# A sum of reciprocals: the last four rows' Exp one row at a time, and the first load in two transfers

## The chip, the cores and the metric

The kernel runs on one core of a Trainium2 chip. The metric is the device time of one execution in microseconds (us). The kernel before takes 171.85 us, the median of three runs that lie between 171.72 and 171.97 us. The profile comes from one further execution, whose span on the core is 169.9 us.

## The reference

The input `x` has the shape 32 x 512 x 1024, float32, all positive: 16,384 rows of 1024 numbers, 67.1 MB. For each row the reciprocals are summed.

```python
x = np.abs(np.random.randn(32, 512, 1024)).astype(np.float32) + 1e-6

def reference(x):
    return np.sum(1.0 / x, axis=-1).astype(np.float32)
```

The 16,384 rows lie as 128 rows on each of the 128 partitions. In the rest of this text, "row c" means the c-th row of every partition, c from 0 to 127: one such row is 128 x 1024 numbers.

## The kernel before

[...] the kernel halves their number. It pairs element i of the first half of a row (call it a) with element i of the second half (b), and uses

1/a + 1/b = (a + b) / (a b).

For each row it forms the 512 products a b, and their reciprocals on ScalarE as exp(-ln(a b)). A power of two, S, is multiplied in twice so that it cancels. What remains is the sum over the pairs of (a + b) times the reciprocal. There are two ways to get it, and the kernel uses both to share the work between engines:

- a row of the "ring" kind: VectorE multiplies the whole row of 1024 by the 512 reciprocals, used twice, and sums up. The reciprocals are the tile `rc` in PSUM.
- a row of the "s" kind: TensorE forms a + b first, as two matmuls with the identity that are accumulated in PSUM (tile `s`), and VectorE multiplies and sums only 512 pairs. The reciprocals are written over the products in the tile `ps`.

The products a b come from GpSimd. For 11 rows TensorE copies the second half to PSUM (tile `b`) and VectorE forms the product.

The work is cut into chunks of two rows. In `(m, e, v)`, m is the number of rows, e how many are of the "s" kind, and v how many products VectorE forms. Chunk A has two ring rows, B two s rows, C two s rows of which VectorE forms one product.

```python
R = 40                                  # rows of the ring buffer in SBUF
A, B, C = (2, 0, 0), (2, 2, 0), (2, 2, 1)
LOADS = [[A, B, A, B], [A, B, A, C]] * 5 + [[A, B], [A, C]] * 4 + [[A], [B], [A], [C]] * 2
```

The loads therefore take eight rows at a time at first, then four, then two. The last four loads are rows 120 and 121 (A), 122 and 123 (B), 124 and 125 (A), 126 and 127 (C).

```python
def sum_rows(c, xc, pr, sm, rc):
    m, e = xc.shape[1], len(sm)
    for j in range(e, m):                           # ring rows
        row = xc[:, j, :].rearrange("p (h e) -> p h e", h=2)
        sum_row(
            c + j,
            row,
            rc[:, j - e, :].unsqueeze(1).to_broadcast([P, 2, H]),
            pr[:, e : e + 2, :] if j == e and m - e > 1 else None,
        )
    for j in reversed(range(e)):                    # s rows, the last one first
        sum_row(c + j, pr[:, j, :], sm[j])

waiting = None
c0 = 0
for chunks in LOADS:
    n = sum(m for m, _, _ in chunks)
    xt = ring[:, c0 % R : c0 % R + n, :]
    keep(nc.sync.dma_start(out=xt, in_=x_v[:, c0 : c0 + n, :]))
    ...                       # for v rows: matmul into b, VectorE product into pr
    for (m, e, v), pr in zip(chunks, made):
        xc = xt[:, q : q + m, :]
        ...                   # GpSimd: the products of rows v to m, into pr
        ...                   # TensorE: s = first half + second half, for e rows
        if waiting:
            sum_rows(*waiting)                      # the chunk before this one
        keep(nc.scalar.activation(out=pr, in_=pr, func=Ln, scale=S))
        rc = None
        if e < m:
            rc = rpool.tile([P, m - e, H], f32, tag="rc")
            i = nc.scalar.activation(out=rc, in_=pr[:, e:, :], func=Exp, scale=-1.0)
            keep(i)
        if e:
            r = pr[:, :e, :]
            keep(nc.scalar.activation(out=r, in_=r, func=Exp, scale=-1.0))
        waiting = c0 + q, xc, pr, sm, rc
        q += m
    c0 += n
sum_rows(*waiting)
nc.sync.dma_start(out=out_v, in_=sums)
```

`keep` holds the instructions of an engine in the order of the program. `sum_row` is one VectorE instruction that multiplies, sums, and writes the elementwise result somewhere; the fourth argument of `sum_row` is that place. For the first ring row of a chunk the place is the tile of products, which Exp has read by then.

Of the kernel before, what the change touches and what calls it, by code (L numbers as in the profile page):

```python
# [1 line left out]

# [6 lines left out]


@with_exitstack
def kernel(
    ctx: ExitStack,
    tc: tile.TileContext,
    x: bass.AP,
    out: bass.AP,
):

    nc = tc.nc
    f32 = mybir.dt.float32
    P = 128  # L30
    D = 1024
    H = D // 2
    F = 128

    R = 40

    S = float(2**17)

    A, B, C = (2, 0, 0), (2, 2, 0), (2, 2, 1)
    LOADS = [[A, B, A, B], [A, B, A, C]] * 5 + [[A, B], [A, C]] * 4 + [[A], [B], [A], [C]] * 2

    Ln = mybir.ActivationFunctionType.Ln
    Exp = mybir.ActivationFunctionType.Exp
    mult = mybir.AluOpType.mult
    plus = mybir.AluOpType.add

    x_v = x.flatten_outer_dims().rearrange("(p f) d -> p f d", p=P)
    out_v = out.flatten().rearrange("(p f) -> p f", p=P)  # L50

    act_sets = list(get_activation_tables(nc.m.arch).keys())
    nc.scalar.add_instruction(  # L53
        mybir.InstLoadActFuncSet(
            name=nc.get_next_instruction_name(),
            act_func_set_id=act_sets.index("natural_log_exp_and_others"),
            ins=[],
            outs=[],
        )
    )  # L60

    ppool = ctx.enter_context(tc.tile_pool(name="ppool", bufs=4))
    opool = ctx.enter_context(tc.tile_pool(name="opool", bufs=1))
    spool = ctx.enter_context(
        tc.tile_pool(name="spool", bufs=3, space=bass.MemoryType.PSUM)
    )
    bpool = ctx.enter_context(
        tc.tile_pool(name="bpool", bufs=1, space=bass.MemoryType.PSUM)
    )
    rpool = ctx.enter_context(  # L70
        tc.tile_pool(name="rpool", bufs=2, space=bass.MemoryType.PSUM)
    )

    ring = opool.tile([P, R, D], f32)
    sums = opool.tile([P, F], f32)
    ident = opool.tile([P, P], f32)
    make_identity(nc, ident)
    keep = tc.keep_in_program_order

    def add(bank, *halves):  # L80
        for k, half in enumerate(halves):
            i = nc.tensor.matmul(  # L82
                bank,
                lhsT=ident,
                rhs=half,
                start=k == 0,
                stop=k == len(halves) - 1,
            )
            keep(i)

    def sum_row(c, row, fac, out=None):
        i = nc.vector.tensor_tensor_reduce(  # L92
            out=row if out is None else out,
            in0=row,
            in1=fac,
            scale=S,
            scalar=0.0,
            op0=mult,
            op1=plus,
            accum_out=sums[:, c : c + 1],  # L100
# [5 lines that stand above are left out]
        for j in range(e, m):  # L106
            row = xc[:, j, :].rearrange("p (h e) -> p h e", h=2)
            sum_row(
                c + j,
                row,  # L110
                rc[:, j - e, :].unsqueeze(1).to_broadcast([P, 2, H]),
                pr[:, e : e + 2, :] if j == e and m - e > 1 else None,
            )
        for j in reversed(range(e)):
            sum_row(c + j, pr[:, j, :], sm[j])

    waiting = None
    c0 = 0
    for chunks in LOADS:
        n = sum(m for m, _, _ in chunks)  # L120
        xt = ring[:, c0 % R : c0 % R + n, :]
        keep(nc.sync.dma_start(out=xt, in_=x_v[:, c0 : c0 + n, :]))  # L122

        made, q = [], 0
        for m, e, v in chunks:
            pr = ppool.tile([P, m, H], f32, tag="ps" if e else "pr")
            for j in range(v):
                b = bpool.tile([P, H], f32, tag="b")
                add(b, xt[:, q + j, H:])
                i = nc.vector.tensor_tensor(  # L130
                    out=pr[:, j, :], in0=xt[:, q + j, :H], in1=b, op=mult
                )
                keep(i)
            made.append(pr)
            q += m

        q = 0
        for (m, e, v), pr in zip(chunks, made):
            xc = xt[:, q : q + m, :]
            if v < m:  # L140
                i = nc.gpsimd.tensor_tensor(  # L141
                    out=pr[:, v:, :], in0=xc[:, v:, :H], in1=xc[:, v:, H:], op=mult
                )
                keep(i)
            sm = []
            for j in range(e):
                s = spool.tile([P, H], f32, tag="s")
                add(s, xc[:, j, :H], xc[:, j, H:])
                sm.append(s)
            if waiting:  # L150
                sum_rows(*waiting)
            keep(nc.scalar.activation(out=pr, in_=pr, func=Ln, scale=S))  # L152
            rc = None
            if e < m:
                rc = rpool.tile([P, m - e, H], f32, tag="rc")
                i = nc.scalar.activation(  # L156
                    out=rc, in_=pr[:, e:, :], func=Exp, scale=-1.0
                )
                keep(i)
            if e:  # L160
                r = pr[:, :e, :]
                keep(nc.scalar.activation(out=r, in_=r, func=Exp, scale=-1.0))  # L162
            waiting = c0 + q, xc, pr, sm, rc
            q += m
        c0 += n
    assert c0 == F, c0
    sum_rows(*waiting)

    nc.sync.dma_start(out=out_v, in_=sums)


# [1 line left out]
_INS = ['x']  # L173
_OUTS = [((32, 512), 'float32')]


# [23 lines left out]
```

## Time and profile before

| | |
|---|---|
| time, median of 3 | 171.85 us |
| span of the profiled execution | 169.9 us |
| TensorE busy | 131.7 us (77%) |
| VectorE busy | 122.3 us (72%) |
| ScalarE busy | 133.9 us (79%) |
| GpSimd busy | 138.3 us (81%) |
| read from HBM | 67.11 MB, in 26 loads of 4, 2 and 1 MB |
| share of the chain that ended last | transfers of x 78%, GpSimd's products 11%, VectorE 3%, ScalarE 2% |

An engine's busy share is an average over the whole execution. The chain that ended last is followed back from the last instruction, at each step to what released it. The views used below are the page's DMA row (the busy share of the 16 DMA engines in 40 equal slices of the span, in tenths), windows (busy time of each engine in chosen stretches, with the granted clock of TensorE, the DMA share and GB/s at the end of the line), and timelines (instructions of one engine in order of time). In the profile PE is TensorE, DVE is VectorE, ACT is ScalarE, POOL is GpSimd. In a timeline, neighbouring instructions of the same kind are put together, and "x2" counts them; a float32 matmul shows as two records.

### The profile page before, as it was taken

How to read it: one execution, taken by the hardware profiler on the slowest of the kernel's cores; microseconds unless marked ns; L12 is line 12 of the kernel's file. 1: busy time of each engine (PE TensorE's matmuls, PEld its weight loads, DVE VectorE, ACT ScalarE, POOL GpSimd, SP SyncE). 2: the span in 40 equal slices, each digit the busy share in tenths (PEclk: the TensorE clock that was granted, in tenths of full speed). 3: DMA queues.
4: the chain of work that ended last, by engine and by line, in shares of the span. 5: the costliest groups of instructions: out<-in, count | busy, mean ns of one | idle time of the engine just before them, and what ended most of it. 6: DMA issues, size and time to landing. Idle time of an engine off the chain costs nothing.

```text
span 169.9 us, 1267 instructions
## 1 busy us (share of the span) xinstructions
PE 131.7 (77%) x278; PEld 50.5 (30%) x278; DVE 122.3 (72%) x267; ACT 133.9 (79%) x129; POOL 138.3 (81%) x70
## 2 busy tenths in 40 slices
PE   0008999786988789784997869789999999888790
PEld 0003433331332233231432323224334342333230
DVE  0000777767987577767777679778989898889883
ACT  3002989978887987958889787999999988999890
POOL 1008999699996999689996998999999889998920
PEclk9999999999999999999999999999999999999999
DMA  6999999999999999999999999999999999999400
GB/s 208 409 455 409 463 409 455 409 463 401 463 411 447 424 440 420 432 434 424 440 424 440 424 397 434 424 428 426 432 428 432 424 413 417 422 420 424 187 0 15
DMA packets 3894, 67.24 MB, mean 396 GB/s; under 512 B 432, under 2 KB 560, under 8 KB 560
## 3 DMA queue, kind: packets, MB, share of 16 engines
q1 hardware_dynamic: 3888, 67.18, 92.9%
q8 instruction: 2, 0.03, 0.1%
q14 instruction: 4, 0.03, 0.0%
HBM read 67.11 MB, written 0.07 MB: 395 GB/s over the span
## 4 chain that ended last, share of the span: by engine, by line
DMA 78%; POOL 11%; DVE 3%; ACT 2%; issue 2%; SPq 1%; POOLq 0%; DVEq 0%
DMA ring<-in_x_dram 78%; POOL pr L141 11%; DVE pr L92 2%; DVE ring L92 1%; ACT pr L152 1%; ACT rc L156 1%; SPq L122 1%; POOLq L141 0%; DVE sums L92 0%; DVEq L92 0%; DVEq L195 0%
## 5 line engine op out<-in xcount | busy, mean ns | idle before, releaser
L141 POOL TENSOR_TENSOR pr<-ring 128x1024 f32<-128x1024 f32 x64 | 137.6, 2189 | 23.6 <-DMA ring<-in_x_dram 23.3
L82 PE MATMUL s<-ring,ident 128*128 128x512 f32 x256 | 122.4, 616 | 32.5 <-DVE sums L92 16.6
L152 ACT ACTIVATE pr<-pr 128x1024 f32<-128x1024 f32 x64 | 67.4, 1053 | 28.7 <-POOL pr L141 28.5
L82 PEld LDWEIGHTS s<-ring,ident 128*128 128x128 f32 x256 | 47.0, 194 | 105.3 <-issue 63.1
L92 DVE CUSTOM_DVE_ANT_1 pr<-ring,rc 128x1024 f32<-128x1024 f32 x32 | 39.1, 1221 | 44.6 <-ACT rc L156 44.6
L92 DVE CUSTOM_DVE_ANT_0 pr<-pr,s 128x512 f32<-128x512 f32 x64 | 41.3, 683 | 0.2
L92 DVE CUSTOM_DVE_ANT_1 ring<-ring,rc 128x1024 f32<-128x1024 f32 x32 | 38.9, 1216 | 0.0
L162 ACT ACTIVATE pr<-pr 128x1024 f32<-128x1024 f32 x32 | 33.8, 1058 | 1.0
L156 ACT ACTIVATE rc<-pr 128x1024 f32<-128x1024 f32 x32 | 32.9, 1028 | 1.0
L82 PE MATMUL b<-ring,ident 128*128 128x512 f32 x22 | 12.0, 626 | 1.4 <-DMA ring<-in_x_dram 1.4
L92 DVE DVE_READ_ACCUMULATOR2_ANT sums<- 128x1 f32 x128 | 10.6, 83 | 0.0
L130 DVE TENSOR_TENSOR pr<-ring,b 128x512 f32<-128x512 f32 x11 | 7.5, 683 | 0.1
L82 PEld LDWEIGHTS b<-ring,ident 128*128 128x128 f32 x22 | 3.5, 188 | 9.0 <-DMA ring<-in_x_dram 7.6
L53 ACT ACT_TABLE_LOAD x1 | 1.3, 1283 | 0.7 <-PEq L184 0.7
masks.py:197 POOL MEMSET ident<- 128x128 f32 x1 | 0.2, 204 | 0.3 <-POOLq L184 0.3
masks.py:199 POOL TENSOR_SCALAR_AFFINE_SELECT ident<-ident 128x128 f32<-128x128 f32 x1 | 0.3, 292 | 0.1
L184 POOL MEMSET const-float32-0.0<- 128x1 f32 x1 | 0.1, 98 | 0.2 <-issue 0.2
L184 POOL MEMSET const-uint8-127<- 128x1 uint8 x1 | 0.1, 103 | 0.0
L184 POOL MEMSET const-bfloat16-1.0<- 128x1 bf16 x1 | 0.1, 101 | 0.0
L184 POOL MEMSET const-float32-1.0<- 128x1 f32 x1 | 0.1, 98 | 0.0
## 6 DMA issues: line engine op xcount, KB each, us to landing
ring<-in_x_dram SPq DMA_DIRECT2D x10, 4096.0 KB, 37.8
ring<-in_x_dram SPq DMA_DIRECT2D x8, 2048.0 KB, 37.0
ring<-in_x_dram SPq DMA_DIRECT2D x8, 1024.0 KB, 28.3
out_dram<-sums SPq DMA_DIRECT2D x1, 64.0 KB, 1.5
```

The costliest lines, as they stand in the source:

```text
L53: nc.scalar.add_instruction(mybir.InstLoadActFuncSet(name=nc.get_next_instruction_name(), act_func_set_id=act_sets.index("natural_log_exp_ ...
L82: i = nc.tensor.matmul(bank, lhsT=ident, rhs=half, start=k == 0, stop=k == len(halves) - 1,)
L92: i = nc.vector.tensor_tensor_reduce(out=row if out is None else out, in0=row, in1=fac, scale=S, scalar=0.0, op0=mult, op1=plus, accum_out ...
L122: keep(nc.sync.dma_start(out=xt, in_=x_v[:, c0 : c0 + n, :]))
L130: i = nc.vector.tensor_tensor(out=pr[:, j, :], in0=xt[:, q + j, :H], in1=b, op=mult)
L141: i = nc.gpsimd.tensor_tensor(out=pr[:, v:, :], in0=xc[:, v:, :H], in1=xc[:, v:, H:], op=mult)
L152: keep(nc.scalar.activation(out=pr, in_=pr, func=Ln, scale=S))
L156: i = nc.scalar.activation(out=rc, in_=pr[:, e:, :], func=Exp, scale=-1.0)
L162: keep(nc.scalar.activation(out=r, in_=r, func=Exp, scale=-1.0))
L184: nc = _bacc.Bacc("TRN2", target_bir_lowering=False, num_devices=1)
```

## The change

It has two parts that have nothing to do with each other.

The first is for the end of the kernel. In the last two chunks, rows 124 to 127, ScalarE forms Exp of one row at a time where it took both rows of a chunk in one instruction, so that VectorE can begin with a row when its own reciprocals are there. For rows 126 and 127 the last row comes first, as VectorE takes them in this order. As Exp of row 125 still has to read its products when VectorE works on row 124, VectorE then writes the elementwise result of row 124 over the row itself and not over the products.

The second is for the start. The first load, of eight rows, is issued as two transfers: partitions 0 to 15 and then partitions 16 to 127. The first transfer is to begin moving data sooner[...]. All later loads stay whole.

```diff
+    SINGLE = 124
...
-                rc[:, j - e, :].unsqueeze(1).to_broadcast([P, 2, H]),
-                pr[:, e : e + 2, :] if j == e and m - e > 1 else None,
+                rc[j - e].unsqueeze(1).to_broadcast([P, 2, H]),
+                pr[:, e : e + 2, :] if j == e and e + 1 < m and c < SINGLE else None,
...
-        keep(nc.sync.dma_start(out=xt, in_=x_v[:, c0 : c0 + n, :]))
+
+        for p0, p1 in ((0, 16), (16, P)) if c0 == 0 else ((0, P),):
+            i = nc.sync.dma_start(out=xt[p0:p1], in_=x_v[p0:p1, c0 : c0 + n, :])
+            keep(i)
...
-            rc = None
-            if e < m:
-                rc = rpool.tile([P, m - e, H], f32, tag="rc")
-                i = nc.scalar.activation(
-                    out=rc, in_=pr[:, e:, :], func=Exp, scale=-1.0
+
+            step = 1 if c0 + q >= SINGLE else m
+            rc = []
+            for j in range(e, m, step):
+                to = min(j + step, m)
+                r = rpool.tile([P, to - j, H], f32, tag="rc")
+                keep(
+                    nc.scalar.activation(
+                        out=r, in_=pr[:, j:to, :], func=Exp, scale=-1.0
+                    )
                 )
-                keep(i)
-            if e:
-                r = pr[:, :e, :]
+                rc += [r[:, l, :] for l in range(to - j)]
+            for to in range(e, 0, -step):
+                r = pr[:, max(to - step, 0) : to, :]
                 keep(nc.scalar.activation(out=r, in_=r, func=Exp, scale=-1.0))
```

## The prediction, made before the changed kernel was run

> **What bounds the kernel now.** I read the page's DMA row first, then the chain that ended last, then the windows of both ends, then each engine's timeline in the last 7 us, since the change touches only the first load and the last four rows.
>
> ```profile
> DMA  6999999999999999999999999999999999999400
> HBM read 67.11 MB, written 0.07 MB: 395 GB/s over the span
> 1.20:1.70 0.50, 0.00 (x0) 0.00 (x0) 0.00 (x0) 0.50 (x1) 0.10 (x1) 1.00 0.00 0
> 1.70:2.00 0.30, 0.00 (x0) 0.00 (x0) 0.00 (x0) 0.30 (x1) 0.00 (x0) 1.00 3.33 874
> 2.00:2.40 0.40, 0.00 (x0) 0.00 (x0) 0.00 (x0) 0.01 (x1) 0.00 (x0) 1.00 0.60 164
> 2.40:2.70 0.30, 0.00 (x0) 0.00 (x0) 0.00 (x0) 0.00 (x0) 0.00 (x0) 1.00 2.25 655
> 23.10:158.60 135.50, 116.20 (x251) 44.42 (x251) 110.25 (x243) 119.82 (x116) 124.57 (x58) 1.00 1.00 428
> 158.60:160.60 2.00, 1.35 (x4) 0.28 (x2) 2.00 (x3) 1.87 (x2) 1.90 (x2) 1.00 0.28 115
> ```
>
> The DMA digits are 9 from the second slice until the data is in: the kernel is bound by its load stream, 428 GB/s in the middle (last column; the column before it is the DMA share, in which a packet counts in the stretch where it starts). The first load is a packet of 32 KB per partition, 128 packets on 16 engines. Bytes by starting stretch: 874 GB/s x 0.30 us = 262 KB, which is 8 packets; 164 x 0.40 = 66 KB, 2 packets; 655 x 0.30 = 197 KB, 6 packets. So the 16 engines start between 1.70 and 2.70 us: ten early, six 0.3 to 0.9 us after the earliest. At the other end the DMA share is 0.28 in 158.60 to 160.60: some engines are done while a few still run, and those few set the last landing.
>
> The timelines of GpSimd, of VectorE and of TensorE (start us, duration us, and in brackets what ended the wait):
>
> ```profile
> 13.45 9.31 POOL L141 TENSOR_TENSOR pr<-ring 128x1024 f32<-128x1024 f32 x4 [12.15 <-DMA ring<-in_x_dram]
> 23.14 4.70 POOL L141 TENSOR_TENSOR pr<-ring 128x1024 f32<-128x1024 f32 x2 [0.38 <-DMA ring<-in_x_dram]
> ...
> 162.26 0.69 DVE L130 TENSOR_TENSOR pr<-ring,b 128x512 f32<-128x512 f32 x1
> 163.32 1.22 DVE L92 CUSTOM_DVE_ANT_1 pr<-ring,rc 128x1024 f32<-128x1024 f32 x1 [0.37 <-ACT rc L156]
> ...
> 165.61 0.08 DVE L92 DVE_READ_ACCUMULATOR2_ANT sums<- 128x1 f32 x1
> 165.84 0.69 DVE L92 CUSTOM_DVE_ANT_0 pr<-pr,s 128x512 f32<-128x512 f32 x1
> ...
> 161.10 1.13 PE L82 MATMUL b<-ring,ident 128*128 128x512 f32 x2 [1.16 <-DMA ring<-in_x_dram]
> 162.06 3.60 PE L82 MATMUL s<-ring,ident 128*128 128x512 f32 x8
> ```
>
> The first load is in at 13.45, the second at 23.14, 9.69 us later, which for 4.19 MB is 433 GB/s. The first took 13.45 - 9.69 = 3.76 us more, of which 0.74 passes before its issue: the start of the stream is what the split is aimed at. At the end the chain runs through GpSimd 158.77, Ln 161.17, Exp 162.26, then VectorE's two rows. But TensorE ends its sums for the last two rows at 162.06 + 3.60 = 165.66, and VectorE's next instruction, which needs the last of them (the sums are consumed last row first), starts at 165.84. VectorE had ended its previous row at 165.69. So two paths arrive 0.03 us apart, and both are released by landings, at 158.7 and 161.1.
>
> [...] The trace of before has no transfer of under 128 partitions[...].
>
> **The change, part by part.**
>
> Exp of rows 124 and 125. [...] VectorE is busy with its product for row 126 until 162.95, so row 124 starts near 162.95 instead of 163.32: 0.37 us earlier, and rows 124 and 125 end near 165.3. [...] But the next VectorE instruction still needs TensorE's sum at 165.66, which no part of this change moves. So about 0.33 of the 0.37 us turns into a wait for TensorE. I leave 0.05 us of gain[...].
>
> Exp of rows 126 and 127. [...] VectorE wants them at 165.8 and 166.4: nothing gained, nothing lost. Row 124's product now goes to its own place in the ring, not to the other buffer; the two forms take 1221 and 1216 ns: no difference.
>
> The split. One more issue of some 0.4 us (the first takes 0.38) is hidden, since an engine's first packet keeps it busy about 1.2 us and more. The first transfer needs one packet for each engine in place of eight. If the stagger of up to 0.9 us is the time in which the packets of an engine after the other are made, it shrinks to about 0.1 us, and the six late engines gain 0.3 to 0.8 us, the others nothing. The stream is without gaps, so an engine keeps what it gained to its last packet. What counts is whether the few engines that land last at 161.1 are among the late starters; the view does not name engines. Half of that, 0.45 us, is my choice.
>
> Sum: 171.85 - 0.45 - 0.05 = 171.35 us.
>
> **The rivals.**
>
> Rival 1, **SBUF ports**: [...] Result 174.7 to 179. [...] The profile of before cannot decide. I give it one chance in four.
>
> Rival 2, **the split is hidden**: the engines that end last are early starters that lost time in mid-stream. Then the landings stay where they are, and only the 0.05 us at the end is left: 171.8. For it: the early group is ten of 16. I give it one in four.
>
> Rival 3, **the Exp split is worth its full 0.37 us**, if TensorE's modelled end is late by so much. Against it: VectorE idled only 0.15 us before 165.84, hence this wait is short now, but its release would not come earlier. With it the sum is 171.0.
>
> **Range and chances.** Without port trouble the time lies between 170.8 (full stagger and part of the Exp) and 171.9. The port rival makes a long upper tail. I choose 170.8 to 177.0, wide upward for that reason alone. 2% is 3.4 us: faster by that has no source in the profile (0.02); slower needs the full port rival (0.24); the rest is the same (0.74).
>
> **What would show it.** Windows of the first microseconds: bytes of all 16 first packets starting in 1.7 to 2.0 means the stagger step is right. First product of GpSimd at 12.9 to 13.5 means no port trouble; at 16 or later, port trouble; and the last TensorE product at 161.1 moves by what the stream won or lost. In the last 5 us: [...] row 124 on VectorE 0.35 us earlier relative to the last landing; and its first product with s still 4.7 us after TensorE's last start for b, with a larger gap before it. If that gap doesn't grow and the product moves earlier, the step that binds it to TensorE is wrong. The prediction is wrong as a whole if the first load's landing moves by more than 1 us.

## The result, and the profile after

The changed kernel takes 180.79 us (median of 4 runs, 180.41 to 181.59) against 171.83 for the kernel before: 1.0527 times as long, with a 95% interval of 1.0489 to 1.0565. It is slower by 9.0 us, more than the predicted range allowed.

The page's DMA rows of the kernel after (busy share of the 16 engines in tenths and GB/s, in 40 slices of 4.5 us), and its list of DMA issues (size, and median us from issue to landing):

```profile
DMA  8989999999999999999999999999999999999500
GB/s 117 235 235 242 308 403 440 455 403 433 462 403 420 462 411 433 451 411 427 440 440 425 425 442 396 414 440 433 412 433 433 422 422 412 422 423 423 225 0 15
...
ring<-in_x_dram SPq DMA_DIRECT2D x1, 3584.0 KB, 21.2
ring<-in_x_dram SPq DMA_DIRECT2D x1, 512.0 KB, 7.1
```

The GB/s row of the kernel before, in slices of 4.2 us:

```profile
GB/s 208 409 455 409 463 409 455 409 463 401 463 411 447 424 440 420 432 434 424 440 424 440 424 397 434 424 428 426 432 428 432 424 413 417 422 420 424 187 0 15
```

Here the reader sees a trap: the engines are as busy as before (8 and 9 in the first five slices), yet move 117 to 308 GB/s where they moved 208 to 463. Busy here is "a packet is under way", not "data flows at full speed". From the sixth slice on the stream runs as before (403 to 462 GB/s in slices 6 to 20, where it was 401 to 463). The timeline of GpSimd after shows when the first and the second load are in (start, duration, and in brackets the wait before it and what ended it):

```profile
22.52 9.31 POOL L145 TENSOR_TENSOR pr<-ring 128x1024 f32<-128x1024 f32 x4 [21.21 <-DMA ring<-in_x_dram]
32.15 4.71 POOL L145 TENSOR_TENSOR pr<-ring 128x1024 f32<-128x1024 f32 x2 [0.32 <-DMA ring<-in_x_dram]
```

The first load is in at 22.52 where it was 13.45: 9.07 us later. The second follows after 9.63 us (9.69 before). So the whole loss lies within the first load, and nothing later makes it good. Windows after, in the stretches that the prediction used (DMA share and GB/s at the end):

```profile
1.70:2.00 0.30, 0.00 (x0) 0.00 (x0) 0.00 (x0) 0.30 (x1) 0.00 (x0) 1.00 9.37 1311
2.00:2.40 0.40, 0.00 (x0) 0.00 (x0) 0.00 (x0) 0.02 (x1) 0.00 (x0) 1.00 0.53 82
2.40:2.70 0.30, 0.00 (x0) 0.00 (x0) 0.00 (x0) 0.00 (x0) 0.00 (x0) 1.00 2.34 328
```

1311 x 0.30 us = 393 KB, 12 first packets; then 1 and 3. It was 8, 2 and 6: more engines do start early. At the other end, VectorE and TensorE after:

```profile
170.96 0.69 DVE L134 TENSOR_TENSOR pr<-ring,b 128x512 f32<-128x512 f32 x1
171.66 1.22 DVE L93 CUSTOM_DVE_ANT_1 ring<-ring,r 128x1024 f32<-128x1024 f32 x1
...
174.50 0.69 DVE L93 CUSTOM_DVE_ANT_0 pr<-pr,s 128x512 f32<-128x512 f32 x1 [0.47 <-PE s L83]
...
169.79 1.12 PE L83 MATMUL b<-ring,ident 128*128 128x512 f32 x2 [1.18 <-DMA ring<-in_x_dram]
170.75 3.60 PE L83 MATMUL s<-ring,ident 128*128 128x512 f32 x8
```

Row 124 (at 171.66) follows the product of row 126 without a gap. Before, VectorE waited 0.37 us there. But now it waits 0.47 us for TensorE before row 127. From TensorE's start for the last landing to that product it is 174.50 - 169.79 = 4.71 us; before it was 165.84 - 161.10 = 4.74.

### The profile page after: what moved, and what is told of

Read it like the earlier page. It is cut to its first block, busy times and chain, and to the rows that moved or that the text cites. A ratio compares the mean times of both kernels' runs of the same rounds, so it can differ in the third digit from the quotient of the medians.

```text
span 178.8 us, 1271 instructions
## 1 busy us (share of the span) xinstructions
PE 131.6 (74%) x278; PEld 50.1 (28%) x278; DVE 122.3 (68%) x267; ACT 134.1 (75%) x131; POOL 138.5 (77%) x70
## 4 chain that ended last, share of the span: by engine, by line
DMA 80%; POOL 9%; PE 3%; issue 2%; ACT 1%; DVE 1%; SPq 1%; DVEq 0%; POOLq 0%
DMA ring<-in_x_dram 80%; POOL pr L145 9%; PE s L83 2%; ACT pr L156 1%; SPq L125 1%; DVE ring L93 1%; PE b L83 1%; DVE pr L93 0%; DVEq L204 0%; ACT pr L171 0%; POOLq L145 0%; DVE sums L93 0%; ACT r L164 0%; DVEq L93 0%
## 5 line engine op out<-in xcount | busy, mean ns | idle before, releaser
L156 ACT ACTIVATE pr<-pr 128x1024 f32<-128x1024 f32 x64 | 67.4, 1052 | 37.4 <-POOL pr L145 37.2
L93 DVE CUSTOM_DVE_ANT_1 pr<-ring,r 128x1024 f32<-128x1024 f32 x31 | 37.9, 1222 | 52.8 <-ACT r L164 52.8
L93 DVE CUSTOM_DVE_ANT_1 ring<-ring,r 128x1024 f32<-128x1024 f32 x33 | 40.1, 1217 | 0.0
L171 ACT ACTIVATE pr<-pr 128x1024 f32<-128x1024 f32 (+1 forms) x33 | 33.9, 1031 | 1.0
L164 ACT ACTIVATE r<-pr 128x1024 f32<-128x1024 f32 (+1 forms) x33 | 33.0, 1001 | 1.0
```

Of the source, the lines that this page charges most:

```text
L93: i = nc.vector.tensor_tensor_reduce(out=row if out is None else out, in0=row, in1=fac, scale=S, scalar=0.0, op0=mult, op1=plus, accum_out ...
L164: nc.scalar.activation(out=r, in_=pr[:, j:to, :], func=Exp, scale=-1.0)
```

## The experiments

The first question was which part costs, and by what mechanism. The first theory was that the rate of a transfer depends on which partitions it reaches; the prediction and the expectations speak of ports. The ports are the author's assumption about the cause: no trace of this case shows one, and what the runs can show is partitions and rates. The rivals were two transfers as such, the uneven cut, and the reading side in HBM. Each edit is to the kernel before, where nothing else is said. Times of single packets of 32 KB are read from the runs' traces.

**The split alone.**

```diff
-        keep(nc.sync.dma_start(out=xt, in_=x_v[:, c0 : c0 + n, :]))
+        for p0, p1 in ((0, 16), (16, P)) if c0 == 0 else ((0, P),):
+            i = nc.sync.dma_start(out=xt[p0:p1], in_=x_v[p0:p1, c0 : c0 + n, :])
+            keep(i)
```

> Only the first load is split (16 and 112 partitions), Exp as before. If the split alone makes the loss: 180.8 us, first product of GpSimd at 22.5 us. If the two parts of the change work on each other: clearly less than 180 us.

Measured: 181.36 us, ratio 1.0523 (1.0478 to 1.0568). The split makes the whole loss. Its window of the start is the clearest for the stagger:

```profile
1.70:2.00 0.30, 0.00 (x0) 0.00 (x0) 0.00 (x0) 0.30 (x1) 0.00 (x0) 1.00 11.71 1638
```

1638 x 0.30 us = 491 KB: 15 of 16 first packets start within 0.3 us. The purpose of the split is reached, and GpSimd's first product still comes at 23.03, 9.6 us late in this trace.

**Two transfers by rows.**

```diff
+        for f0, f1 in ((0, 4), (4, 8)) if c0 == 0 else ((0, n),):
+            ... out=xt[:, f0:f1, :], in_=x_v[:, c0 + f0 : c0 + f1, :]
```

> The first load in two transfers as well, but by rows: four rows and four rows, each on all 128 partitions. If the loss comes from the partitions that a transfer reaches (theory of the ports): no loss, 171.5 to 172.2 us, second half landed at 13.4. If two transfers in place of one are what costs: several us slower, 175 or more.

Measured: 172.10 us, ratio 1.0005 (0.9982 to 1.0029). Two transfers in place of one cost nothing if each has all 128 partitions. The rival "two transfers as such" falls. GpSimd's product of the second half:

```profile
13.07 4.68 POOL L145 TENSOR_TENSOR pr<-ring 128x1024 f32<-128x1024 f32 x2 [0.22 <-DMA ring<-in_x_dram]
```

So the whole load is in 0.38 us earlier than before (13.45), and the time is no shorter: TensorE's last product for `b` starts at 161.09, where it was 161.10.

**Two halves of the partitions.** The pieces are `((0, 64), (64, P))`.

> The first load in two transfers of 64 partitions (0 to 63, 64 to 127)[...]. Theory of the ports: [...] the load takes twice 9.7 us, the first product of GpSimd comes at about 23.2 us and the time is about 181.5 us. If it is the uneven cut (1 and 7 packets to an engine) or the small first transfer that costs: about 172 us.

Measured: 182.37 us, ratio 1.0606 (1.0583 to 1.0629), first product of GpSimd at 23.96. An even cut loses more than the uneven one: 182.37 us against 181.36. The window over the load:

```profile
3.60:23.90 20.30, 0.00 (x0) 0.00 (x0) 0.00 (x0) 0.00 (x0) 0.00 (x0) 1.00 0.97 213
```

The whole load before:

```profile
3.60:13.40 9.80, 0.00 (x0) 0.00 (x0) 0.00 (x0) 0.00 (x0) 0.00 (x0) 1.00 1.00 431
```

213 GB/s is half of 431. In the trace 89 of the load's 128 packets of 32 KB take 2.5 to 2.6 us, where in the whole load most take 1.21.

**The same cut with another source.** The transfers of 16 and 112 partitions read the first 1024 rows of x, one after the other; the first eight rows of every partition then hold sums of other rows than the reference's.

```diff
+            near = x.flatten_outer_dims()[0:1024].rearrange("(p f) d -> p f d", p=P)
+            for p0, p1 in ((0, 16), (16, P)):
+                keep(nc.sync.dma_start(out=xt[p0:p1], in_=near[p0:p1]))
```

> Split of 16 and 112 partitions as in the change, but the first load reads other rows of x: the first 1024 rows one after the other, 32 KB from partition to partition in HBM where it was 512 KB (the first eight rows of every partition are then sums of other rows than the reference's). If the loss is on the side of SBUF (ports): 180.8 us as with the split alone. If it is on the side of HBM, from 16 engines that read at a distance of 512 KB in step: about 172 us.

Measured: 180.90 us, ratio 1.0518 (1.0491 to 1.0545), first product at 22.49. Where the data lies in HBM made no difference. The distance of 512 KB between the partitions' data is not the cause.

**The split in mid-stream.** The same cut at rows 24 to 31.

```diff
+        for p0, p1 in ((0, 16), (16, P)) if c0 == 24 else ((0, P),):
```

> The split of 16 and 112 partitions at the fourth load (rows 24 to 31) in place of the first. Theory of the ports: the stream stands just as long, some 9 us, for the load is slow wherever it lies: 180 to 181 us, because nothing later in the stream makes the time good. If the loss belongs to the start (first bytes, empty queues): about 172 us.

Measured: 184.35 us, ratio 1.0731 (1.0712 to 1.0750). It isn't the start that matters. The loss is larger than expected, 12.5 us. GpSimd's timeline shows where:

```profile
35.46 9.33 POOL L143 TENSOR_TENSOR pr<-ring 128x1024 f32<-128x1024 f32 x4 [4.06 <-DVE sums L92]
54.72 7.00 POOL L143 TENSOR_TENSOR pr<-ring 128x1024 f32<-128x1024 f32 x3 [9.94 <-DMA ring<-in_x_dram]
```

The same two before:

```profile
32.92 9.34 POOL L141 TENSOR_TENSOR pr<-ring 128x1024 f32<-128x1024 f32 x4 [1.52 <-DMA ring<-in_x_dram]
42.63 8.26 POOL L141 TENSOR_TENSOR pr<-ring 128x1024 f32<-128x1024 f32 x4 [0.37 <-DMA ring<-in_x_dram]
```

The first bracket after names VectorE, but the load ahead of the cut was itself in no earlier: its last piece lands at 35.32 us in the trace. So the load with the cut takes 19.26 us from the one before it (9.71 without the cut), which is 9.55 us lost, and the load ahead of it is 2.54 us later already; the remaining 0.4 us were not traced. In the trace the last five packets of that load take 1.5 to 2.5 us instead of 1.21. The small transfer may hold them up, but that was not shown. Of the 16-partition transfer's packets, eight take 4.6 to 4.9 us here, four times 1.21, and eight take 3.3 to 4.1.

**Three pieces, the first of them from the middle.** The pieces are `((32, 96), (0, 32), (96, P))`.

> The first load in three transfers: partitions 32 to 95, then 0 to 31, then 96 to 127. [...] Theory of the ports: the 64 in the middle go at the full rate, 2.1 MB in some 4.9 us, the other two at half, 1.05 MB in 4.9 us each; first product of GpSimd at about 18.3 us and the time about 176.8 us. If any transfer of fewer than 128 partitions is slow (the halves went at half rate): the load takes about 19.5 us as with the halves, first product near 23 us, time near 182 us.

Measured: 179.09 us, ratio 1.0412 (1.0372 to 1.0453). The load's stretches:

```profile
3.60:7.00 3.40, 0.00 (x0) 0.00 (x0) 0.00 (x0) 0.00 (x0) 0.00 (x0) 1.00 0.95 405
7.00:12.80 5.80, 0.00 (x0) 0.00 (x0) 0.00 (x0) 0.00 (x0) 0.00 (x0) 1.00 1.12 266
12.80:18.50 5.70, 0.00 (x0) 0.00 (x0) 0.00 (x0) 0.00 (x0) 0.00 (x0) 1.00 0.92 218
```

This is the run that decides. 64 partitions from 32 to 95 go at close to the full rate, 405 GB/s in 3.60 to 7.00 against 431 for the whole load before: after the first, their packets take 1.2 to 1.4 us in the trace. In the same kernel the 32 at either end go at half rate, 218 GB/s in 12.80 to 18.50: 53 of their 64 packets take 2.3 to 2.6 us (the middle stretch above mixes the tail of the fast piece with the slow one). So "fewer than 128 partitions" is not slow in itself; which partitions they are decides, in this kernel. First product at 19.61, expected 18.3; the time is 2.3 us over the expected 176.8. A little of that is the start: the first packets begin at 2.16 us instead of 1.75. The traced execution was the shortest of the four, 177.86 us.

**The other order.** The pieces are `((16, P), (0, 16))`.

> The same two transfers in the other order, 112 partitions (16 to 127) first and then 16 (0 to 15). Theory of the ports: the 112 are as slow as before[...], and the 16 take four times a packet's 1.21 us, so the loss is of the same kind, 7 to 10 us, 179 to 182 us. If a small transfer at the very start is what holds the queues up: 172 to 173 us.

Measured: 181.84 us, ratio 1.0567 (1.0521 to 1.0612), first product at 22.90. The list of DMA issues:

```profile
ring<-in_x_dram SPq DMA_DIRECT2D x1, 3584.0 KB, 18.6
```

The 112 partitions are in at 0.74 + 18.6 = 19.3 us, with no small transfer ahead of them; seven eighths of a whole load would be in at 13.45 - 9.69 / 8 = 12.2 (an estimate from the landings before). The packets of the 16 take 3.3 to 4.5 us. Both pieces are slow in either order.

**Exp alone.** The second question was the end. This is the change with its first load whole.

```diff
-        for p0, p1 in ((0, 16), (16, P)) if c0 == 0 else ((0, P),):
+        for p0, p1 in ((0, P),):
```

(Here the lines taken away are those of the changed kernel.)

> Only Exp of the last four rows one at a time; the first load whole. If TensorE's last sum holds VectorE back (the step in the prediction): 171.75 to 171.85 us, VectorE's wait before its first product with s of row 127 grows to about 0.5 us. If Exp was the bound: 171.4 to 171.5 us.

Measured: 171.88 us against 171.81, ratio 1.0006 (0.9999 to 1.0012). Nothing is gained. VectorE's timeline:

```profile
163.25 1.22 DVE L93 CUSTOM_DVE_ANT_1 ring<-ring,r 128x1024 f32<-128x1024 f32 x1
164.40 1.22 DVE L93 CUSTOM_DVE_ANT_1 ring<-ring,r 128x1024 f32<-128x1024 f32 x1
...
166.07 0.69 DVE L93 CUSTOM_DVE_ANT_0 pr<-pr,s 128x512 f32<-128x512 f32 x1 [0.45 <-PE s L83]
166.68 0.68 DVE L93 CUSTOM_DVE_ANT_0 pr<-pr,s 128x512 f32<-128x512 f32 x1
```

**Exp, and row 126 before row 127.** To show that TensorE's last sum holds the end, take away what makes VectorE need it first. This is an edit to the Exp-only kernel.

```diff
-        for j in reversed(range(e)):
+        for j in range(e) if c >= SINGLE else reversed(range(e)):
             sum_row(c + j, pr[:, j, :], sm[j])
...
-            for to in range(e, 0, -step):
-                r = pr[:, max(to - step, 0) : to, :]
+            for j in range(0, e, step):
+                r = pr[:, j : min(j + step, e), :]
```

> As the Exp-only kernel, and in the last chunk row 126 comes before row 127, on ScalarE and on VectorE, in the order in which TensorE makes their sums. If TensorE's last sum is the bound, row 126 no longer waits for it: VectorE runs through, and the end comes about 0.45 us earlier, 171.4 us. If Exp split alone has gained already, or the end is set elsewhere: no difference to the Exp-only kernel.

Measured: 171.23 us, ratio 0.9969 (0.9958 to 0.9981). It beats both kernels, by 0.6 us and by 9.6. VectorE's timeline:

```profile
163.19 1.22 DVE L93 CUSTOM_DVE_ANT_1 ring<-ring,r 128x1024 f32<-128x1024 f32 x1
...
164.33 1.22 DVE L93 CUSTOM_DVE_ANT_1 ring<-ring,r 128x1024 f32<-128x1024 f32 x1
...
165.48 0.68 DVE L93 CUSTOM_DVE_ANT_0 pr<-pr,s 128x512 f32<-128x512 f32 x1
...
166.08 0.68 DVE L93 CUSTOM_DVE_ANT_0 pr<-pr,s 128x512 f32<-128x512 f32 x1
```

The wait is gone: row 126 starts as soon as row 125 is done, and the last product starts at 166.08 where it was 166.68 in the Exp-only kernel.

**The order alone.** `for j in range(e) if c >= 124 else reversed(range(e))` in the kernel before, Exp whole.

> The kernel before with row 126 before row 127 at the end, Exp not split. Here VectorE is free at 165.69 and TensorE done at 165.66: only the start after the wait can gain, 0.1 to 0.2 us, 171.65 to 171.75 us. If TensorE were the whole bound of the end without any help of Exp: 0.4 us or more.

Measured: 171.57 us, ratio 0.9990 (0.9981 to 0.9999). In its trace row 126 is taken first, at 165.59, where row 127 started at 165.84. Alone, the order is worth some 0.2 us and Exp nothing; together 0.6 us. Each removes one of the two paths that arrived at the same time.

## Why the prediction was wrong, point by point

**What bounds the kernel: right.** The load stream is the bound, and what it loses at its start (9.07 us) comes out at the end (9.0 us).

**The stagger: right in part.** Eight of the 16 first packets started after 2.00 us before, four in the changed kernel and one in the run with the split alone; the prediction's own sign was all 16 by 2.00. The step that followed, "an engine keeps what it gained to its last packet", took each engine's speed as given. It is not: the first packets, which took 1.6 to 2.2 us before, take 2.8 to 4.5 us in the changed kernel. Nor is a gain at the start sure to reach the end: the 0.38 us of the cut by rows did not.

**The choice against the port rival: this is the step that failed.** The prediction named the rival, gave it one chance in four, and put its central time on the other side: the first load 0.45 us earlier, where it came 9.07 us later. Its range ended at 177.0, inside the rival's own 174.7 to 179. What spoke for the other side was the author's assumption that partitions are tied to engines, so that a small transfer would keep only a few of them busy; no trace showed such a tie. The runs contradict it for these transfers. In the changed kernel the 16 packets of the small transfer all start by 2.63 us, before one of them ends (4.62): 16 engines take one each, not a few engines several. The 112 that follow then each start within 0.02 us of the end of another packet, in 16 chains of seven (the whole load before makes 16 chains of eight). With the halves, such a tie would leave each packet its 1.21 us; 89 of 128 took 2.5 to 2.6. What the runs show is which partitions were slow: both halves at 213 GB/s against 431, and the 64 in the middle at 405. Why they differ was not shown.

**The size of the rival: mis-sized.** The rival's 174.7 to 179 lies 2.9 to 7.2 us over 171.85, and no run had shown what it was built on; 9.0 us were lost. The small transfer is in at 0.74 + 7.1 = 7.8 us. An eighth of the load before would be in at 13.45 - 7/8 x 9.69 = 5.0 (an estimate from the landings). So 2.8 us are lost there. In the trace its packets run from 1.76 to 6.48 us: 524 KB in 4.7 us, 111 GB/s. The larger part is that of the 112 partitions. From 7.8 to 22.5 they take 14.7 us, where 7/8 of 9.69 is 8.5: 6.2 us are lost, by a factor of 14.7 / 8.5 = 1.7.

Why these 112 are slow stays open, and it is two thirds of the loss. In the trace all 112 packets are slow, 1.5 to 3.3 us with a median of 2.1, where most of the whole load's took 1.21. Which partitions each engine took was not seen.

**Exp: right, by its own step.** The prediction said "about 0.33 of the 0.37 us turns into a wait for TensorE": the wait grew from 0.15 us to 0.45 us, and the Exp-only kernel gained nothing. In the changed kernel row 124 starts 1.87 us after TensorE's start for the last landing (171.66 - 169.79), where it was 2.22 (163.32 - 161.10): 0.35 us earlier, as forecast. The 0.05 us set down as a gain was not seen. Two Exp of 512 took 1.12 us in all for rows 124 and 125, 0.60 and 0.58 by themselves, where one of 1024 took 1.03 before. That the first is done when VectorE comes free was the author's estimate; it ended at 170.93 + 0.60 = 171.53, and VectorE's product for row 126 at 170.96 + 0.69 = 171.65. Rival 3 falls with the Exp-only run. Rival 2, a split that changes nothing, was not met.

## What to carry to other kernels

If a load like this one is to be cut, cut it along its rows, not along its partitions. The same data cut in halves by rows cost nothing (172.10 us, ratio 1.0005), and cut in halves by partitions 10 us (182.37 us, ratio 1.0606), with DMA engines that look just as busy (share 0.97 in the window of the load against 1.00). Partitions 0 to 15 ran at 111 GB/s and the halves at 213, where the whole load ran at 431; the 64 in the middle kept 405, but the 112 took 14.7 us for 3.67 MB, 250 GB/s (an estimate from the landings). And where two paths end together, as here, shortening one gains nothing (171.88 us with Exp alone against 171.81): look for what the next instruction needs after the one that you release, and change the order so that the last thing made is the last thing needed (171.23 us).

## What was not expected of the hardware

Issuing a transfer of 64 partitions held the queue for 0.57 us (halves) and 0.64 us (middle piece), against 0.38 us for 128 partitions, 0.39 for 16 and 0.40 for 112, each from one trace. Its first packets began at 2.1 us, 0.35 us later. Why is open.
